# Transposing softmax tiles by VectorE's 32x32 blocks and a round trip through DRAM, in a two-layer decoder trunk

## The chip, the cores and the metric

The kernel runs on one core of a Trainium2 chip. The metric is the device time of one execution in microseconds (us), lower is better. Beside three timed runs there is one profiled execution; all rows below are of that one.

## What is computed

Two layers of a decoder over 256 positions of width 2048, in float32. Each layer has one input projection, several groups of attention heads side by side, a gate and an output projection; 256 memory tokens are attended to as well. The part that matters here is what every head does:

```python
s = jnp.einsum('bhqd,bhkd->bhqk', qi, k).astype(jnp.float32) * scale
s = jnp.where(kpos[None, :] <= qpos[:, None], s, -jnp.inf)
p = jax.nn.softmax(s, axis=-1).astype(v.dtype)
return jnp.einsum('bhqk,bhkd->bhqd', p, v)
```

Layer 0 has 8 latent-attention (MLA) heads, 8 block-sparse (MoBA) heads and 4 memory heads; layer 1 has 16 sliding-window heads with sinks, 6 dilated heads and 4 memory heads. With 256 positions, MoBA's one block is the whole sequence, so those heads are plain causal ones.

## The kernel before, in words

**Weights.** All weight matrices lie in one DRAM array in 332 pieces of up to 512 KB, in the order of use. A piece is loaded on SP's queue into one of RB = 4 `raw` buffers (`issue`, L337), rounded by ScalarE into `hi` (L424) and completed by VectorE with `lo` = raw - hi (L429), into one of HB = 4 pairs. `step` (L538) is the main loop: it converts ahead by AHEAD = 3 pieces (`ensure`), issues the products of half a piece, calls `run_bg` once, and does the same with the second half. A product of a 128x128 weight block is one matmul of `hi` with 512 columns and one of `lo` with 256 (L580, L581); for the projections with the weights as moving operand it is three (L603 to L605).

**Background work.** Everything else, attention included, is written as Python generators. `run_bg` (L495) advances every active generator to its next `yield`, so the `yield`s fix the order of the instructions on each engine. One call of `run_bg` is called a tick here: one half of a piece. At most four queued heads are active together, and a new one starts at the earliest every 5 (later 6) ticks.

**A head.** `g_causal` (L933) makes the scores of a head into one PSUM bank, 384 columns wide: queries 0 to 127 against keys 0 to 127, and queries 128 to 255 against all 256 keys. `g_softmax` (L815) adds the mask and takes the maximum (DVE, L822), the exponential with its sum (ACT, L832), the reciprocal (L839), and scales the two parts (ACT L842, DVE L843). `g_transposed` (L848) transposes the three 128x128 blocks on TensorE with the identity (L850) back into the same bank; ACT rounds two blocks to `hi` in a `PT` buffer (L862) and copies the third (L864), DVE makes `lo` (L866). `pv_causal` (L901) multiplies by the values: three matmuls of 256 columns (L899) and one of 128 in full float32 (L903). `g_meet` (L488) lets a head wait up to 10 ticks so that its PE work falls together with another head's scores.

`g_swa` (L966) does two sliding-window tiles at once (8 such pairs), `g_mem` (L1008) a memory head with four blocks (8 heads). So 38 tiles of three blocks and 8 of four are transposed. `Val` (L905) holds the values of a group of heads; `V.drop` gives them back.

The order on a queue is the order of the code. SP's queue holds the weight loads, each of which waits for DVE's L429 to free a `raw` buffer.

Of the kernel before, what the change touches and what calls it, by code (L numbers as in the profile page):

```python
# [10 lines left out]
F32 = mybir.dt.float32  # L11
# [209 lines left out]
def body(ctx, tc, xr, xT, memT, memr, wall, gains, fing, sinks, consts, out):  # L221
    nc = tc.nc
# [588 lines left out]

    CUTS3 = (slice(0, 128), slice(128, 384))
    CUTS2 = (slice(0, 256), slice(256, 512))

    def g_softmax(sc, cuts, mask, scale, sink, P):  # L815
        s = wtile("st", 8, 16)
        if mask is None:
            nc.vector.tensor_reduce(s[:, 0:2], sc.rearrange("p (t k) -> p t k", t=2),
                                    axis=mybir.AxisListType.X, op=OP.max)
        else:  # L820
            for t, c in enumerate(cuts):
                nc.vector.tensor_tensor_reduce(P[:, c], sc[:, c], mask[:, c], 1.0, -3.0e38, OP.add, OP.max,  # L822
                                               s[:, t:t + 1])
# [5 lines left out]
        yield  # L829
        src = sc if mask is None else P  # L830
        for t, c in enumerate(cuts):
            nc.scalar.activation(P[:, c], src[:, c], AF.Exp, bias=s[:, 2 + t:3 + t], scale=scale,  # L832
                                 accum_out=s[:, 4 + t:5 + t])
# [71 lines left out]
    class Val:  # L905
# [3 lines left out]
        def __init__(self, n, mem=False, u=None):  # L909
            self.n, self.ready, self.given = n, True, u is not None  # L910
            self.us = [u] if self.given else [vr.get() for _ in range(1 + mem)]
            self.parts = [(u[:, 0:512], u[:, 512:1024]) for u in self.us]
            self.second = None if mem else big.get()

# [18 lines left out]
    def g_causal(kt, raws, pe, V, vo, mask, scale, free):  # L933
# [32 lines left out]
    def g_swa(j, q, kc, scale):  # L966
# [22 lines left out]
        while len(ptp.free) < 2:  # L989
            yield  # L990
        PT = [ptp.get() for s in range(2)]
        gs = [g_transposed(P[s], B[s], (0, 1, 2), PT[s], T) for s in range(2)]
        for _ in range(4):
            for g in gs:
                next(g)
            yield
        for s in range(2):
            pv3(B[0][:, 0:256], (vzr[:, 0, s], vzr[:, 1, s]), T[s][0:2], s == 0, False)
        for s in range(2):
            nc.tensor.matmul(B[0][:, 128:256], vz[:, s], T[s][2], start=False, stop=s == 1, skip_group_check=True)  # L1000
        banks.put(B[1])
        for s in range(2):
            pp.put(P[s])
            ptp.put(PT[s])
        yield
        yield from g_finish(j, B[0])

    def g_mem(kt, q, k, V, vo, layer1=False):  # L1008
# [10 lines left out]
        else:  # L1019
            km_drop()  # L1020
        while not (banks.free and pp.free):
            yield
        b, P = banks.get(), pp.get()
        for t in range(2):
# [3 lines left out]
        yield  # L1028
        yield from g_softmax(b, CUTS2, None, 128.0 ** -0.5, None, P)
        while not ptp.free:  # L1030
            yield
        T, PT = [], ptp.get()
        yield from g_transposed(P, b, (0, 2, 1, 3), PT, T)
# [3 lines left out]
        pp.put(P)  # L1037
        ptp.put(PT)
        V.drop()
# [8 lines left out]
    def v_evac(V, c0=0, n=512, r=None):  # L1048
        def evac(m, cur):
            src = [p[:, c0:c0 + n] for p in cur]  # L1050
            hi, lo = (v[:, 0:n] for v in V.parts[0])
# [11 lines left out]

    def vm_split(V, src):
        for t in range(2):
# [169 lines left out]
    def mla_group(g):  # L1235
        V = Val(4)
        h0 = 4 * g
# [168 lines left out]
    def g_last(t, p, lag):  # L1406
# [4 lines left out]
        s = wtile("st", 8, 16)  # L1411
        q = pp.get()
# [3 lines left out]
        nc.scalar.activation(q[:, lo], x[:, lo], AF.Square, accum_out=ss[:, t, 3:4])  # L1416
        nc.vector.tensor_tensor_reduce(q[:, hi], x[:, hi], x[:, hi], 1.0, 0.0, OP.mult, OP.add, ss[:, t, 4:5])
        nc.vector.tensor_reduce(s[:, 0:1], ss[:, t, :], axis=mybir.AxisListType.X, op=OP.add)
# [101 lines left out]
```

## Time and profile before

| what | value |
|---|---|
| three timed runs, median (lowest to highest) | 1004.75 us (1004.57 to 1005.36) |
| the profiled execution, its own time | 1004.67 us |
| its span, first to last instruction | 1002.6 us |
| granted TensorE clock, mean of full speed | 0.999 |
| HBM traffic | 189.38 MB read, 4.19 MB written |

PE stands for TensorE's matmuls, PEld for its weight loads, DVE for VectorE, ACT for ScalarE, POOL for GpSimd, SP for SyncE, which issues DMAs. Matmuls overlap in the pipeline, so the duration of one is longer than the time until the next can start; the pace is read from start to start. Names such as `at` (attention banks in PSUM), `mm` (products of weights) and `P` (score tiles) are the program's, with buffer numbers left out. A line number is that of the kernel before; with the change, the lines behind L271 are higher by 2 and more.

### The profile page before, as it was taken

The numbers are of one execution on the slowest core, as the hardware profiler recorded it, in microseconds if no ns is written. First come the engines' busy times: TensorE is split into PE (matmuls) and PEld (weight loads), VectorE is DVE, ScalarE is ACT, GpSimd is POOL, SyncE is SP. The second block draws the span as 40 slices with busy tenths as digits, with TensorE's granted clock in tenths as the row PEclk, the third lists the DMA queues.
The fourth block names the chain that finished last, engine by engine and source line by source line (L and its number), as shares of the span: only waits on it lengthen the run. The fifth ranks groups of instructions, "written<-read, shape, count | busy, mean of one in ns | idle before, by whom it ended". The sixth has DMA issues, their size and how long they took to land.

```text
span 1002.6 us, 15260 instructions
## 1 busy us (share of the span) xinstructions
PE 993.3 (99%) x5519; PEld 865.2 (86%) x5519; DVE 679.9 (68%) x1326; ACT 602.6 (60%) x1175; POOL 174.0 (17%) x155
## 2 busy tenths in 40 slices
PE   9999999999999999999999999999999999999996
PEld 8888988888888888888888888888899888888885
DVE  7756886887785687765556756777766668666543
ACT  7776776776555456655545555577776565665441
POOL 0000222230241232100000000232211343221110
PEclk9999999999999999999999999999999999999999
DMA  9887455454555555668766554544446555568732
GB/s 337 318 292 246 133 167 187 147 168 168 170 168 171 185 169 170 208 233 268 260 218 231 170 179 168 169 157 158 158 120 201 173 181 165 168 230 282 259 124 84
DMA packets 56093, 194.57 MB, mean 194 GB/s; under 512 B 6481, under 2 KB 8529, under 8 KB 56017
## 3 DMA queue, kind: packets, MB, share of 16 engines
q1 hardware_dynamic: 55296, 192.77, 58.0%
q8 instruction: 43, 0.70, 0.3%
q10 hardware_dynamic: 720, 0.82, 0.2%
q14 instruction: 34, 0.27, 0.1%
HBM read 189.38 MB, written 4.19 MB: 193 GB/s over the span
## 4 chain that ended last, share of the span: by engine, by line
PE 99%; DVE 0%; issue 0%; ACT 0%; DVEq 0%
PE mm L580 38%; PE mm L581 19%; PE mm L603 10%; PE mm L605 10%; PE mm L604 10%; PE at L899 2%; PE at L890 2%; PE at L850 2%; PE at L894 1%; PE mm L1466 1%; PE mm L1464 1%; PE mm L1465 1%; PE at L903 0%; PE at L1079 0%; PE at L1000 0%; PE at L737 0%
## 5 line engine op out<-in xcount | busy, mean ns | idle before, releaser
L429 DVE TENSOR_TENSOR lo<-raw,hi 128x1024 fp32r<-128x1024 f32 (+2 forms) x325 | 394.8, 1217 | 151.9 <-ACT hi L424 147.4
L424 ACT ACTIVATE hi<-raw 128x1024 fp32r<-128x1024 f32 (+2 forms) x325 | 340.5, 1050 | 150.5 <-PE mm L605 103.9
L580 PE MATMUL mm<-bufB,hi 128*128 128x512 f32 x816 | 288.9, 396 | 0.0
L580 PE MATMUL mm<-bufA,hi 128*128 128x512 f32 x816 | 286.5, 394 | 0.0
L581 PE MATMUL mm<-bufB,lo 128*128 128x256 f32 x816 | 229.4, 281 | 0.0
L581 PE MATMUL mm<-bufA,lo 128*128 128x256 f32 x816 | 228.4, 280 | 0.0
L580 PEld LDWEIGHTS mm<-bufB,hi 128*128 128x128 f32 x816 | 154.2, 189 | 34.1 <-ACT hi L398 0.2
L580 PEld LDWEIGHTS mm<-bufA,hi 128*128 128x128 f32 x816 | 153.3, 188 | 32.7
L581 PEld LDWEIGHTS mm<-bufB,lo 128*128 128x128 f32 x816 | 154.3, 189 | 1.0 <-DVE lo L399 0.6
L581 PEld LDWEIGHTS mm<-bufA,lo 128*128 128x128 f32 x816 | 153.4, 188 | 0.2
L603 PE MATMUL mm<-hi,bufB 128*128 128x512 f32 (+1 forms) x264 | 101.7, 385 | 0.0
L604 PE MATMUL mm<-lo,bufB 128*128 128x512 f32 (+1 forms) x264 | 101.2, 383 | 0.0
L605 PE MATMUL mm<-hi,bufB 128*128 128x512 f32 (+1 forms) x264 | 101.1, 383 | 0.0
L616 ACT ACTIVATE tmp<-mm 128x256 f32<-128x256 f32 x118 | 45.1, 382 | 88.8 <-PE mm L581 87.0
L603 PE MATMUL mm<-hi,bufA 128*128 128x512 f32 x204 | 79.8, 391 | 0.0
L604 PE MATMUL mm<-lo,bufA 128*128 128x512 f32 x204 | 79.5, 390 | 0.0
L605 PE MATMUL mm<-hi,bufA 128*128 128x512 f32 x204 | 79.5, 390 | 0.0
L634 POOL TENSOR_TENSOR qk<-qk,cst 32x256 f32<-32x256 f32 x28 | 48.9, 1747 | 162.4 <-DVE rope L633 150.1
L794 POOL TENSOR_TENSOR gf<-gf,qk 128x256 f32<-128x256 f32 x28 | 36.5, 1304 | 159.2 <-ACT e L789 159.2
L605 PEld LDWEIGHTS mm<-hi,bufB 128*128 128x128 f32 x264 | 49.6, 188 | 9.2
L603 PEld LDWEIGHTS mm<-hi,bufB 128*128 128x128 f32 x264 | 49.6, 188 | 9.0
L604 PEld LDWEIGHTS mm<-lo,bufB 128*128 128x128 f32 x264 | 49.6, 188 | 8.6
(188 smaller groups left out, 1101.3 us busy)
## 6 DMA issues: line engine op xcount, KB each, us to landing
raw<-in_wall SPq DMA_DIRECT2D x321, 512.0 KB, 3.5
raw<-in_wall SPq DMA_DIRECT2D x8, 384.0 KB, 3.1
big<-in_xT SPq DMA_DIRECT2D x4, 512.0 KB, 6.3
raw<-in_xr SPq DMA_DIRECT2D x4, 512.0 KB, 5.2
raw<-in_memr SPq DMA_DIRECT2D x4, 512.0 KB, 4.4
big<-in_xr SPq DMA_DIRECT2D x4, 512.0 KB, 5.9
raw<-in_memT SPq DMA_DIRECT2D x4, 512.0 KB, 3.9
x1d<-big SPq DMA_DIRECT2D x4, 512.0 KB, 5.6
```

What stands on the lines that cost most here:

```text
L424: nc.scalar.activation(hi[:, c], raw[:, c], AF.Copy)
L429: nc.vector.tensor_tensor(lo[:, c], raw[:, c], hi[:, c].bitcast(F32), op=OP.subtract)
L580: nc.tensor.matmul(p, hi[:, c], x, start=kt == 0, stop=False, skip_group_check=True)
L581: nc.tensor.matmul(p[:, 0:256], lo[:, c], x[:, 0:256], start=False, stop=last, skip_group_check=True)
L603: nc.tensor.matmul(p, xh, hi[:, w], start=kt == 0, stop=False, skip_group_check=True)
L604: nc.tensor.matmul(p, xh, lo[:, w], start=False, stop=False, skip_group_check=True)
L605: nc.tensor.matmul(p, xl, hi[:, w], start=False, stop=kt == g.kt - 1, skip_group_check=True)
L616: nc.scalar.activation(t, p[:, 256:512], AF.Copy)
L634: nc.gpsimd.tensor_tensor(t[0:n], t[0:n], cs[0:n], op=OP.mult)
L794: nc.gpsimd.tensor_tensor(gf, gf, o_, op=OP.mult)
L850: nc.tensor.transpose(pt[:, 128 * dst:128 * dst + 128], P[:, 128 * b:128 * b + 128], ident)
L890: nc.tensor.matmul(o, q[:, a + q0:a + q0 + 128], k[:, b:b + 256], start=first and i == 0, stop=last and i == 2, skip_group_check=True)
```

## The change

The transposes on TensorE go. The scores' bank is given back as soon as the exponential has read it or the masked scores have been written to `P`. Then, for each tile:

- the scale by 1/sum writes not back into `P` but into one shared tile `W`, in a column order (`keys`, `laid`) that puts key 4i + b of a block into block b's column i;
- DVE transposes `W` in 32x32 blocks into `P` (`g_turn`);
- SP stores `P` to one of 8 DRAM buffers `pd`, and three ticks later loads it back so that each group of 32 partitions is spread over the 128, in four pieces a row;
- four ticks later ACT rounds two blocks from `P` to `hi` in `PT`, DVE makes `lo`, both from SBUF instead of PSUM; the third block is used by the product straight from `P`, as four runs of 32 columns.

A memory head uses two tiles of 256 columns instead of one of 512. The pools change: `P` from 5 of 512 columns to 7 of 384, `PT` from 4 to 3. The values' buffers are taken by `Val.take` only when the values are written, and the first MLA group's lie in a free part of `bufB`. The final normalization uses two `P` tiles where it used one. The core of the diff, without `Val`, the rest of `g_swa`, `g_mem` and `g_last`:

```diff
@@ -269,11 +269,13 @@
     vr = Free("vr", 2, [128, 1024], dt=F32R)
     spl = Free("spl", NSPL, [128, 512], dt=F32R)
     osg = qk
-    pp = Free("P", 5, [128, 512], work)
-    ptp = Free("PT", 4, [128, 512], work, F32R)
+    pp = Free("P", 7, [128, 384], work)
+    ptp = Free("PT", 3, [128, 512], work, F32R)
     banks = Free("at", 4, [128, 512], ps)
     ident = cst[:, C_ID:C_ID + 128]
     x1d = dram.tile([4, 128, 1024], F32, name="x1d")
+    pw = Free("W", 1, [128, 384], work)
+    pds = Free("pd", 8, [128 * 384], dram)
     def wtile(tag, n=256, bufs=2):
         return (small if n < 256 else work).tile([128, n], F32, name=tag, tag=tag, bufs=bufs)
@@ -837,33 +839,86 @@
         if sink is not None:
             nc.vector.tensor_tensor(s[:, 4:6], s[:, 4:6], s[:, 6:8], op=OP.add)
         nc.vector.reciprocal(s[:, 6:8], s[:, 4:6])
-        yield
-        c0, c1 = cuts
-        nc.scalar.activation(P[:, c1], P[:, c1], AF.Copy, scale=s[:, 7:8])
-        nc.vector.tensor_scalar(P[:, c0], P[:, c0], s[:, 6:7], None, op0=OP.mult)
-        yield
-        yield
-        yield
-    def g_transposed(P, pt, blocks, T, out):
-        for dst, b in enumerate(blocks):
-            nc.tensor.transpose(pt[:, 128 * dst:128 * dst + 128], P[:, 128 * b:128 * b + 128], ident)
-        n = 128 * len(blocks)
-        if n == 512:
-            while not spl.free:
+        yield s[:, 6:8]
+    def laid(w, n):
+        return w.rearrange("p (b s i) -> p s b i", b=4, s=n)
+    def keys(P):
+        return P.rearrange("p (s i b) -> p s b i", b=4, i=32)
+    def g_turn(P, W, n):
+        nc.vector.transpose(P[:, 0:128 * n], W)
+        yield
+        d = pds.get()
+        c = d[0:128 * 128 * n]
+        nc.sync.dma_start(c.rearrange("(p f) -> p f", p=128), P[:, 0:128 * n])
+        for _ in range(3):
+            yield
+        nc.sync.dma_start(P[:, 0:128 * n].rearrange("p (a f) -> p a f", a=4),
+                          c.rearrange("(a p f) -> p a f", a=4, p=128))
+        pds.put(d)
+        for _ in range(4):
+            yield
+    def g_causal_T(P, r, out):
+        while not pw.free:
+            yield
+        w = pw.get()
+        nc.scalar.activation(laid(w, 3)[:, 1:3], keys(P[:, 128:384]), AF.Copy, scale=r[:, 1:2])
+        nc.vector.tensor_scalar(laid(w, 3)[:, 0], keys(P[:, 0:128])[:, 0], r[:, 0:1], None, op0=OP.mult)
+        yield
+        pw.put(w)
+        yield from g_turn(P, w, 3)
+        while not ptp.free:
+            yield
+        PT = ptp.get()
+        hi, lo = PT[:, 0:256], PT[:, 256:512]
+        p = P.rearrange("p (a s j) -> p s a j", a=4, s=3)
+        parts = [v.rearrange("p (s a j) -> p s a j", a=4, s=2) for v in (hi, lo)]
+        out.append((hi, lo, p[:, 2], PT))
+        nc.scalar.activation(parts[0], p[:, 0:2], AF.Copy)
+        yield
+        nc.vector.tensor_tensor(parts[1], p[:, 0:2], parts[0].bitcast(F32), op=OP.subtract)
+        yield
+        yield
+    def g_mem_T(P, r, out):
+        gs = []
+        for t in range(2):
+            while not pw.free:
                 yield
-            hi, lo = T, spl.get()
-            out.append((hi, lo))
-        else:
-            hi, lo = T[:, 0:256], T[:, 256:512]
-            out.append((hi, lo, P[:, 256:n]))
-        m = hi.shape[-1]
-        yield
-        nc.scalar.activation(hi, pt[:, 0:m], AF.Copy)
-        if m < n:
-            nc.scalar.activation(P[:, m:n], pt[:, m:n], AF.Copy)
-        yield
-        nc.vector.tensor_tensor(lo, pt[:, 0:m], hi.bitcast(F32), op=OP.subtract)
+            w = pw.get()
+            if t:
+                nc.scalar.activation(laid(w[:, 0:256], 2), keys(P[t][:, 0:256]), AF.Copy, scale=r[:, 1:2])
+            else:
+                nc.vector.tensor_scalar(laid(w[:, 0:256], 2), keys(P[t][:, 0:256]), r[:, 0:1], None, op0=OP.mult)
+            yield
+            pw.put(w)
+            gs.append(g_turn(P[t], w[:, 0:256], 2))
+            next(gs[t])
+        for i in range(9):
+            for g in gs:
+                next(g, None)
+            if i < 8:
+                yield
+        while not (ptp.free and spl.free):
+            yield
+        hi, lo = ptp.get(), spl.get()
+        p = [P[t][:, 0:256].rearrange("p (a s j) -> p s a j", a=4, s=2) for t in range(2)]
+        parts = [v.rearrange("p (s t a j) -> p t s a j", t=2, s=2, a=4) for v in (hi, lo)]
+        out.append((hi, lo))
+        for t in range(2):
+            nc.scalar.activation(parts[0][:, t], p[t], AF.Copy)
+        yield
+        for t in range(2):
+            nc.vector.tensor_tensor(parts[1][:, t], p[t], parts[0][:, t].bitcast(F32), op=OP.subtract)
         yield
         yield
...
@@ -949,16 +1010,19 @@
         for t in free:
             qk.put(t)
         yield
-        yield from g_softmax(b, CUTS3, mask, scale, None, P)
+        T = []
+        for r in g_softmax(b, mask, scale, None, cuts3(P)):
+            if r is None:
+                yield
+        banks.put(b)
+        yield from g_causal_T(P, r, T)
         yield from g_meet()
-        while not ptp.free:
-            yield
-        T, PT = [], ptp.get()
-        yield from g_transposed(P, b, (0, 1, 2), PT, T)
-        yield from g_meet()
+        while not banks.free:
+            yield
+        b = banks.get()
         pv_causal(b, V.head(vo), T[0])
         pp.put(P)
-        ptp.put(PT)
+        ptp.put(T[0][3])
         V.drop()
         yield
         yield from g_finish(kt, b)
...
@@ -980,30 +1044,32 @@
         spl.put(R[0])
         qk.put(q)
         yield
-        gs = [g_softmax(B[s], CUTS3, lay[:, 512:896], scale, j + 8 * s, P[s]) for s in range(2)]
-        for _ in range(6):
-            for g in gs:
-                next(g)
...
```

**PE's queue, in the first MLA group**, before. `at` are attention banks, `P` score tiles, `bufB,hi` and `bufB,lo` weight products; L850 are the transposes of two heads, L894 and L890 the scores of the third:

```order
L580 MATMUL mm<-bufB,hi 128x512
L581 MATMUL mm<-bufB,lo 128x256
L850 MATMUL at_125<-cst,P_117 128x128 x3
L850 MATMUL at_123<-cst,P_113 128x128 x3
L894 MATMUL at_124<-qk_92,qk_94 128x128
L894 MATMUL at_124<-qk_97,qk_98 128x128
L890 MATMUL at_124<-spl_112,spl_111 128x256 x3
L890 MATMUL at_124<-bufA,spl_109 128x256 x3
L580 MATMUL mm<-bufB,hi 128x512
```

And with the change, the scores of the same third head:

```order
L582 MATMUL mm<-bufB,hi 128x512
L583 MATMUL mm<-bufB,lo 128x256
L949 MATMUL at_125<-qk_92,qk_94 128x128
L949 MATMUL at_125<-qk_97,qk_95 128x128
L945 MATMUL at_125<-spl_111,spl_109 128x256 x3
L945 MATMUL at_125<-bufA,spl_112 128x256 x3
L582 MATMUL mm<-bufB,hi 128x512
```

The six transposes are gone, and the weight products go on right behind the scores. (Lines 580 and 581 are now 582 and 583, L894 and L890 are L949 and L945.)

**SP's queue with the change, in the MoBA heads.** `pd` is DRAM; a row with x3 is three loads of weight pieces:

```order
L339 DMA raw<-in_wall 128x1024 x7
L859 DMA pd_129<-P_115 128x384
L339 DMA raw<-in_wall 128x1024
L862 DMA P_115<-pd_129 128x4x96
L339 DMA raw<-in_wall 128x1024 x3
L859 DMA pd_130<-P_116 128x384
L339 DMA raw<-in_wall 128x1024
L862 DMA P_116<-pd_130 128x4x96
```

Before there were only weight loads here. Each store (L859) now has one weight load between itself and the load back (L862), and three weight loads stand behind that one before the next head's store.

## Rows read from the trace of the kernel before

**Rows 1.** The page: the span, and each engine's busy time, share and instructions.

```profile
span 1002.6 us, 15260 instructions
...
PE 993.3 (99%) x5519; PEld 865.2 (86%) x5519; DVE 679.9 (68%) x1326; ACT 602.6 (60%) x1175; POOL 174.0 (17%) x155
```

**Rows 2.** The chain that ended last, whole span: shares by line.

```profile
by line: PE mm L580 37.7%; PE mm L581 19.2%; PE mm L603 10.5%; PE mm L605 10.4%; PE mm L604 10.4%; PE at L899 1.9%; PE at L890 1.9%; PE at L850 1.6%; PE at L894 1.0%; PE mm L1466 0.8%; PE mm L1464 0.8%; PE mm L1465 0.8%; PE at L903 0.5%; PE
```

**Rows 3.** Waits of PE: who waited for whom, us in total, times, longest.

```profile
PE at L1079 <- DVE ones L1073: 1.0, 1, 1.0
```

**Rows 4.** PE's timeline from 200 us: start us, us, engine, line, operation.

```profile
203.27 0.39 PE L580 MATMUL mm<-bufB,hi 128*128 128x512 f32 x1
...
204.66 0.39 PE L580 MATMUL mm<-bufB,hi 128*128 128x512 f32 x1
```

**Rows 5.** L850: count, ns min/median/max, first and last start us.

```profile
L850 PE MATMUL at<-cst,P x146: 270/273/273, 118.7 to 894.1; 128*128 128x128 f32 x146
```

**Rows 6.** The chain by time, two stretches: start us, us, what.

```profile
191.66 0.65 PE at L850 x6
...
200.41 0.36 PE at L899 x3
201.00 0.36 PE at L899 x3
...
353.42 0.36 PE at L899 x3
...
365.69 0.33 PE at L850 x3
```

**Rows 7.** Lines by form, costliest first: busy us, mean ns, idle before.

```profile
L429 DVE TENSOR_TENSOR lo<-raw,hi 128x1024 fp32r<-128x1024 f32 x315 | 385.8, 1227 | 148.8 <-ACT hi L424 144.2 <-PE mm L580 2.8
L424 ACT ACTIVATE hi<-raw 128x1024 fp32r<-128x1024 f32 x315 | 332.6, 1058 | 149.7 <-PE mm L605 103.9 <-PE mm L580 36.6 <-DMA raw<-in_wall 4.1
...
L842 ACT ACTIVATE P<-P,st 128x256 f32<-128x256 f32 x46 | 22.3, 503 | 4.3 <-DVE st L839 3.4
...
L822 DVE CUSTOM_DVE_ANT_0 P<-at,lay 128x256 f32<-128x256 f32 x38 | 15.9, 420 | 0.0
...
L866 DVE TENSOR_TENSOR PT<-at,PT 128x256 fp32r<-128x256 f32 x38 | 14.9, 416 | 0.9 <-ACT P L864 0.7
L862 ACT ACTIVATE PT<-at 128x256 fp32r<-128x256 f32 x38 | 14.7, 386 | 24.8 <-PE at L850 24.8
...
L822 DVE CUSTOM_DVE_ANT_0 P<-at,lay 128x128 f32<-128x128 f32 x38 | 11.0, 290 | 39.7 <-PE at L890 39.7
...
L864 ACT ACTIVATE P<-at 128x128 f32<-128x128 f32 x38 | 10.7, 281 | 0.0
...
L633 DVE STREAM_SHUFFLE rope<-qk 128x256 f32<-128x256 f32 x14 | 6.2, 446 | 0.0
```

**Rows 8.** Busy us by stretch: PE, PEld, DVE, ACT, POOL, PE clock, DMA share, GB/s.

```profile
200.00:300.00 100.00, 100.00 (x589) 88.46 (x588) 76.36 (x175) 61.18 (x133) 25.69 (x21) 1.00 0.52 169
650.00:780.00 130.00, 130.00 (x829) 116.53 (x828) 92.26 (x254) 90.14 (x226) 32.10 (x26) 1.00 0.51 160
```

**Rows 9.** DMA: queues (packets, MB, share), then issues (count, KB, us to landing).

```profile
q1 hardware_dynamic: 55296, 192.77, 58.0%
...
q10 hardware_dynamic: 720, 0.82, 0.2%
...
raw<-in_wall SPq DMA_DIRECT2D x321, 512.0 KB, 3.5
...
big<-in_memT SPq DMA_DIRECT2D x3, 512.0 KB, 6.5
...
out<-big SPq DMA_DIRECT2D x6, 128.0 KB, 2.5
```

**Rows 10.** Waits of all engines, longest first in total.

```profile
ACT hi L424 <- PE mm L605: 103.9, 79, 1.7
...
ACT hi L424 <- DMA raw<-in_wall: 4.7, 6, 2.0
```

More of the change, by code (lines that the diff above doesn't have):

```diff
@@ L810, in gate_evac, with cuts3, g_softmax @@
         return evac
-    CUTS3 = (slice(0, 128), slice(128, 384))
-    CUTS2 = (slice(0, 256), slice(256, 512))
-    def g_softmax(sc, cuts, mask, scale, sink, P):
+    def cuts3(P):
+        return [(c, P[:, c]) for c in (slice(0, 128), slice(128, 384))]
+    def g_softmax(sc, mask, scale, sink, Ps):
         s = wtile("st", 8, 16)
@@ L820, in g_softmax @@
         else:
-            for t, c in enumerate(cuts):
-                nc.vector.tensor_tensor_reduce(P[:, c], sc[:, c], mask[:, c], 1.0, -3.0e38, OP.add, OP.max,
+            for t, (c, P) in enumerate(Ps):
+                nc.vector.tensor_tensor_reduce(P, sc[:, c], mask[:, c], 1.0, -3.0e38, OP.add, OP.max,
                                                s[:, t:t + 1])
@@ L829, in g_softmax @@
         yield
-        src = sc if mask is None else P
-        for t, c in enumerate(cuts):
-            nc.scalar.activation(P[:, c], src[:, c], AF.Exp, bias=s[:, 2 + t:3 + t], scale=scale,
+        for t, (c, P) in enumerate(Ps):
+            nc.scalar.activation(P, sc[:, c] if mask is None else P, AF.Exp, bias=s[:, 2 + t:3 + t], scale=scale,
                                  accum_out=s[:, 4 + t:5 + t])
@@ L909, in __init__, with take @@
         def __init__(self, n, mem=False, u=None):
-            self.n, self.ready, self.given = n, True, u is not None
-            self.us = [u] if self.given else [vr.get() for _ in range(1 + mem)]
+            self.n, self.ready, self.given, self.mem = n, True, u is not None, mem
+            self.us = [u] if self.given else []
+        def take(self):
+            while len(vr.free) + len(self.us) < 1 + self.mem or not (self.mem or big.free):
+                yield
+            while len(self.us) < 1 + self.mem:
+                self.us.append(vr.get())
             self.parts = [(u[:, 0:512], u[:, 512:1024]) for u in self.us]
-            self.second = None if mem else big.get()
+            self.second = None if self.mem else big.get()
         def head(self, c):
@@ L982, in g_swa @@
         yield
-        gs = [g_softmax(B[s], CUTS3, lay[:, 512:896], scale, j + 8 * s, P[s]) for s in range(2)]
-        for _ in range(6):
-            for g in gs:
-                next(g)
+        gs = [g_softmax(B[s], lay[:, 512:896], scale, j + 8 * s, cuts3(P[s])) for s in range(2)]
+        for i in range(3):
+            r = [next(g) for g in gs]
+            if i < 2:
+                yield
+        for b in B:
+            banks.put(b)
+        for s in range(2):
+            launch(g_causal_T(P[s], r[s], T))
+        while len(T) < 2:
+            yield
+        for _ in range(3):
             yield
         yield from g_meet()
-        while len(ptp.free) < 2:
+        while not banks.free:
             yield
[L991 to L995, printed above, removed]
-            yield
+        b = banks.get()
         for s in range(2):
-            pv3(B[0][:, 0:256], (vzr[:, 0, s], vzr[:, 1, s]), T[s][0:2], s == 0, False)
+            pv3(b[:, 0:256], (vzr[:, 0, s], vzr[:, 1, s]), T[s][0:2], s == 0, False)
         for s in range(2):
-            nc.tensor.matmul(B[0][:, 128:256], vz[:, s], T[s][2], start=False, stop=s == 1, skip_group_check=True)
-        banks.put(B[1])
+            nc.tensor.matmul(b[:, 128:256], vz[:, s], T[s][2], start=False, stop=s == 1, skip_group_check=True)
         for s in range(2):
             pp.put(P[s])
-            ptp.put(PT[s])
+            ptp.put(T[s][3])
         yield
-        yield from g_finish(j, B[0])
+        yield from g_finish(j, b)
     def g_mem(kt, q, k, V, vo, layer1=False):
@@ L1020, in g_mem @@
             km_drop()
-        while not (banks.free and pp.free):
+        while not banks.free or len(pp.free) < 2:
             yield
-        b, P = banks.get(), pp.get()
+        b, P = banks.get(), [pp.get(), pp.get()]
         for t in range(2):
@@ L1028, in g_mem @@
         yield
-        yield from g_softmax(b, CUTS2, None, 128.0 ** -0.5, None, P)
-        while not ptp.free:
+        T = []
+        Ps = [(slice(256 * t, 256 * t + 256), P[t][:, 0:256]) for t in range(2)]
+        for r in g_softmax(b, None, 128.0 ** -0.5, None, Ps):
+            if r is None:
+                yield
+        banks.put(b)
+        yield from g_mem_T(P, r, T)
+        while not banks.free:
             yield
-        T, PT = [], ptp.get()
-        yield from g_transposed(P, b, (0, 2, 1, 3), PT, T)
+        b = banks.get()
         for h in range(2):
@@ L1036, in g_mem @@
         spl.put(T[0][1])
-        pp.put(P)
-        ptp.put(PT)
+        for p in P:
+            pp.put(p)
+        ptp.put(T[0][0])
         V.drop()
@@ L1049, in evac @@
         def evac(m, cur):
+            yield from V.take()
             src = [p[:, c0:c0 + n] for p in cur]
@@ L1064, in vm_split @@
     def vm_split(V, src):
+        yield from V.take()
         for t in range(2):
@@ L1415, in g_last @@
             nc.vector.tensor_tensor(x[:, c], p[:, c], x[:, c], op=OP.add)
-        nc.scalar.activation(q[:, lo], x[:, lo], AF.Square, accum_out=ss[:, t, 3:4])
-        nc.vector.tensor_tensor_reduce(q[:, hi], x[:, hi], x[:, hi], 1.0, 0.0, OP.mult, OP.add, ss[:, t, 4:5])
+        nc.scalar.activation(q, x[:, lo], AF.Square, accum_out=ss[:, t, 3:4])
+        nc.vector.tensor_tensor_reduce(q1, x[:, hi], x[:, hi], 1.0, 0.0, OP.mult, OP.add, ss[:, t, 4:5])
         nc.vector.tensor_reduce(s[:, 0:1], ss[:, t, :], axis=mybir.AxisListType.X, op=OP.add)
```

4 lines of the change are left out of this document (2 added, 2 removed).

## The prediction

> **What bounds the kernel now.** I read the profile from the top down: the engines' busy time, the chain that ended last, the waits of the engine that the chain names, and then the places that the change touches. TensorE (PE) is busy 993.3 us of the 1002.6 us span, VectorE (DVE) 68%, ScalarE (ACT) 60% [rows 1]. The chain is PE for 99%; 88% of it, by five lines, is the weight products, and the transposes of L850 have 1.6% [rows 2]. PE's list of waits holds one entry, of 1.0 us at the start [rows 3]. So from start to tail PE runs one instruction after another, and the time is the sum of what PE issues. A product of a piece (512 columns, then 256) starts every 0.35 us: four pairs from 203.27 to 204.66 [rows 4]. That is 1.39 us for half a piece, which is one turn of the background generators; I call it a tick. Inserted attention products lengthen a tick, so 1.39 us is its lower bound.
>
> **What is removed.** 38 score tiles of three blocks (22 causal heads, 16 sliding-window tiles) and 8 memory tiles of four are transposed: 38 x 3 + 8 x 4 = 146, the count in the trace [rows 5]. The 273 ns there is no price: it contains the pipeline. The chain shows the pace: six take 0.65 us, three 0.33 us [rows 6]. That is 0.11 us each, 146 x 0.11 = 16.0 us; the chain's 1.6% of 1002.6 us gives the same. Nothing covers these on PE, and all lie on the path. The order of PE with the change is otherwise that of before: as many weight products, nowhere a longer run of attention work without them, and the queue of heads ends earlier.
>
> **What is added.** (1) DVE: 38 block transposes of 384 columns and 16 of 256. The nearest row is the shuffle of 128x256, 446 ns; two rows of L822 grow by 130 ns for 128 columns more, so 384 take about 0.58 us [rows 7]. Sum 38 x 0.58 + 16 x 0.45 = 29 us. Bounds: nothing below the 290 ns of a 128-column operation (16 us), and twice the estimate above (58 us). I take 29, as the shuffle is nearest in kind. (2) The scale by 1/sum now writes W in another column order, reading every fourth element: between ACT's 503 ns of today [rows 7] and twice that, 38 x 0.5 = 19 us more on ACT over the kernel. I take no more, since the count of elements is the same. (3) ACT loses 38 copies of the third block, 281 ns each, 10.7 us [rows 7]. All this lies beside PE: in the stretch from 200 to 300 us DVE has 24 us idle of 100 and ACT 39, in the sliding-window stretch 38 and 40 of 130 [rows 8]. Seven heads in the first of them add 4 us to DVE, 8 us at the upper bound. Cost on the path: nothing, as long as PE's operands are ready. (4) The third block is now read by PE as four runs of 32 columns. The trace has no such operand; that product takes 0.23 us now (from 200.77 to 201.00) [rows 6]. Bounds: nothing, and one more of the same for 38 products, 8.7 us; no row gives a reason for a gain. I take nothing, as equal columns have cost equal time in every row.
>
> **The round trip.** 54 stores of 196 or 131 KB, and 54 loads that cut each row into four pieces of 384 or 256 B: 128 and 512 packets. All go on SP's queue among the weight loads. A store waits for its block transpose; the load waits until the store has landed, and whatever stands behind it on SP waits too. From the code, the load is issued three ticks behind the store, ACT's copy of the loaded tile comes four ticks behind the load, the product that uses it three ticks later: ten ticks, at least 13.9 us, in causal and memory heads, three more in a sliding-window pair.
>
> No DRAM round trip of this kind stands in the trace. The landings nearest in bytes are 2.5 us (128 KB out) and the longest of common ones 6.5 us (512 KB in) [rows 9]. With ACT's copy and DVE's subtraction (0.4 us each [rows 7]) two landings come to 5.8 to 13.8 us, under the 13.9 at both ends; I take 2.5 and 3.5 us, 6.8 us. While SP stands at the load, weight loads stand behind it; their margin comes next. ACT works ahead of PE: it converts piece i+3 during step i and is held by PE, 103.9 us at one line, against 4.7 us by weight DMA [rows 10]. Of the three pieces ahead, 8.3 us, a conversion takes 2.3 (L424, L429 [rows 7]). So ACT can stand still for some 6 us before PE lacks weights, and a raw buffer's refill (3.5 us [rows 9]) has about as much to spare.
>
> Packets: the 55,296 on q1 took 58.0% of 16 engines' span, 168 ns each at 3.5 KB; the 720 on q10, of 1.1 KB, 45 ns each [rows 9]. A load of 512 packets takes 512 x 45 / 16 = 1.4 us of all engines at the lower price and 5.4 us at the upper one. I take 45 ns: the pieces are nearer to 1.1 KB. A causal head comes every 12.3 us (353.42 to 365.69 [rows 6]); the DMA is busy half of that [rows 8], and gets 1.4 us plus about 0.4 for the store: under 70%. At 168 ns (5.4 and 1.3 us) the transfers come to 13 of 12.3 us, saturated. The Trainium skill speaks against such pieces: "DMA: Bandwidth & Descriptors", Specifications, gives 512 B as the least transfer at line rate, with a read-modify-write below. By the 45 ns of the row the sum is 988.7 us; by the rule, taken as hard as the row of the long packets allows, it is the second rival's 1015.7. No run here shows it yet.
>
> **Sum.** 1004.67 us of the profiled execution (0.08 below the median of the runs) minus 16.0 = 988.7 us. The 2.1 us outside the span, PE's start and the tail behind its last product stay.
>
> **Rivals.**
> - *Part of the gain is lost* (chance 0.16, of which 0.02 ends within 0.2%). PE now waits a little where it does not wait today: the strided operand costs up to 8.7 us, or weights come late after SP stood at a load. With 38 groups of tiles, 0.2 us each is 7.6 us: 996 us. For it: PE has no other slack than what ACT and DVE work ahead. Against: PE waits for nobody today, and ACT hardly for weights [rows 3, 10].
> - *The round trip is too long* (0.12, slower). The place is the product behind the copy of the loaded tile, in the 30 causal and memory heads. It decides from two landings together of 13.1 us on, which a saturated DMA at 168 ns a packet would give. At 7 us each the product waits 0.9 us, 30 x 0.9 = 27 us: 1015.7 us. Break-even is 16.0 / 30 = 0.53 us of wait per head. ACT, standing at the copy, would also hold up the weights. Against: the DMA was idle 48% of these stretches, and weight loads landed in 3.5 us there.
> - *The change does not reach PE* (0.02, within 0.2%). The gaps that transposes filled reappear as waits of the same products. Against: PE's order has weight products there, whose weights lie ready: 1004.7 us.
>
> **Numbers.** Forecast 988.7 us, chance 0.70, by itself 986 to 991: below, if PE's pace in a transpose also cost neighbours up to 0.02 us; above, for a first few waits. Left: 0.16, 0.12 and 0.02. A difference of 0.2% (2 us) is what a measurement can tell here. Faster: 0.70 + 0.14 = 0.84. Same: 0.02 + 0.02 = 0.04. Slower: 0.12. The range goes from 986 to 1000 us, taking in the strided operand's upper bound and the 0.2 us waits, and leaves out the slow rival, the unchanged one and a little of the second.
>
> **What would show it.** Right: the transposes' 1.6% gone from the chain, PE's waits still about 1 us, the load's landing under 5 us, ACT's wait for the loaded tile small, DVE near 710 us and ACT near 590 us busy. Wrong: PE waiting for DVE or ACT at L899 or L903 (their new numbers), weight conversions waiting for DMA far above 4.7 us, landings of 7 us or more, a DMA share near full in the attention stretches, or a product of 128 columns of well over 0.23 us.

## The result, and the profile after

The changed kernel takes 990.4 us (median of four runs, 990.09 to 990.49) against 1004.77 us (1004.57 to 1005.36) before: a ratio of 0.9855 [0.9838, 0.9873]. It is 14.4 us faster, and 1.7 us above the 988.7 us forecast. The profiled execution took 990.38 us.

The page of the changed kernel: span, busy times, the weight queue, HBM traffic. It answers to [rows 1, 9].

```profile
span 988.6 us, 15244 instructions
...
PE 976.3 (99%) x5373; PEld 847.4 (86%) x5373; DVE 718.2 (73%) x1388; ACT 605.0 (61%) x1137; POOL 169.3 (17%) x155
...
q1 hardware_dynamic: 91584, 211.92, 66.0%
...
HBM read 198.95 MB, written 13.76 MB: 215 GB/s over the span
```

PE issues 146 instructions less and is busy 17.0 us less, but the span is only 14.0 us shorter: 3.0 us more of it are gaps. PE's waits in the changed kernel (who for whom: us in total, times, longest), which answer to [rows 3], say where:

```profile
PE at L1153 <- DVE ones L1147: 1.0, 1, 1.0
PE mm L582 <- ACT hi L400: 0.7, 2, 0.5
PE mm L583 <- DVE lo L431: 0.6, 1, 0.6
PE mm L582 <- ACT big L1127: 0.6, 1, 0.6
PE at L954 <- DVE spl L921: 0.6, 1, 0.6
PE mm L583 <- DVE lo L401: 0.5, 2, 0.2
```

The first was there before. Those at L400, L401 and L431 lie in the first 14 us, among the first weights; they came out larger or smaller in every kernel below. The other two are new: L954 at 133.6 us, L1127 at 190.3 us. Behind them PE has no listed wait to its last product. The chain that ended last, 99% PE before, is now 93% PE: it leaves PE in the first 14 us and on its way to both places.

**A balance by stages.** Three PE instructions are the same in every version: the first product that broadcasts a statistic (L667 before, L669 now), the first transpose of the residual at the layer boundary (L737, L739), and the last product of the program. The first two enclose layer 0 with 64 of the 146 transposes (16 heads of three, 4 of four), the last two layer 1 with 82. Their start times in PE's timeline, in us:

| kernel | statistic | boundary | last product | layer 0 | layer 1 |
|---|---|---|---|---|---|
| before | 71.28 | 544.99 | 994.00 | 473.71 | 449.01 |
| after | 71.49 | 540.23 | 980.08 | 468.74 | 439.85 |
| only PE's transposes left out (e1) | 71.38 | 538.74 | 978.59 | 467.36 | 439.85 |
| memory heads two ticks later (e6) | 71.40 | 539.01 | 978.84 | 467.61 | 439.83 |
| and causal scale a tick later (e10) | 71.52 | 538.24 | 978.07 | 466.72 | 439.83 |

Layer 1 gains 9.16 us, 0.112 us for each of its transposes, and loses nothing: the same 439.85 as with the transposes simply left out. Layer 0 gains 4.97 us where 64 x 0.11 = 7.0 were due. The 2 us that are missing lie at the two new waits and at a shorter stand behind the first, as e6 and e10 below show by taking them away.

**The two waits.** ACT's timeline of the changed kernel around the second (start us, us, engine, line, operation, idle before and its releaser), then PE's and DVE's around both, from the same view:

```profile
186.98 0.76 ACT L873 ACTIVATE W<-P,st 128x256 f32<-128x256 f32 x1 [2.22 <-DVE st L841]
...
190.06 0.58 ACT L1127 ACTIVATE vr<-mm 128x512 fp32r<-128x512 f32 x1
...
190.28 0.28 PE L583 MATMUL mm<-bufB,lo 128*128 128x256 f32 x1
191.18 0.50 PE L582 MATMUL mm<-bufB,hi 128*128 128x512 f32 x1 [0.62 <-ACT big L1127]
191.52 0.28 PE L583 MATMUL mm<-bufB,lo 128*128 128x256 f32 x1
...
131.31 1.41 DVE L628 TENSOR_TENSOR bufA<-qk,bufA 64x256 fp32r<-64x256 f32 x2
132.75 0.76 DVE L921 TENSOR_TENSOR spl<-P,PT 128x256 fp32r<-128x256 f32 x2
...
132.73 0.28 PE L954 MATMUL at<-PT,vr 128*128 128x256 f32 x1
133.57 0.39 PE L954 MATMUL at<-spl,vr 128*128 128x256 f32 x1 [0.55 <-DVE spl L921]
...
142.64 0.28 PE L954 MATMUL at<-PT,vr 128*128 128x256 f32 x1
143.01 0.39 PE L954 MATMUL at<-spl,vr 128*128 128x256 f32 x1
```

At 186.98 ACT's scale (L873) had stood 2.22 us for DVE's reciprocal (L841). Before, a `yield` lay between the two, and the scale waited 0.57 us for it; the diff removes that `yield`. Behind the scale on ACT comes the eviction of the value products (L1127), 1.5 us later than before (190.06 against 188.56), and PE waits for the PSUM bank that it empties. At 132.75 DVE makes the low parts of a memory head (L921), late behind L628, in two operations that take 0.76 us together; PE has begun the product that needs them. DVE is nearly full here: busy 22.4 of the 23 us from 121 to 144 us, against 20.4 before.

The list counts a wait from the end of the instruction before it. From start to start more is lost. Behind 190.28 the next product starts 0.90 us later instead of 0.12, and the one after that 0.34 instead of 0.23: 0.9 us. At 132.73 the next start comes 0.84 us later instead of 0.12, with 0.1 more behind it: 0.8 us. The next memory head loses another 0.35 us in the same way at 142.64, which is too short for the list.

**The added work by line.** Lines by form (busy us, mean ns; idle before):

```profile
L873 ACT ACTIVATE W<-P,st 128x256 f32<-128x256 f32 x38 | 28.6, 753 | 22.1 <-DVE st L841 12.8 <-DVE P L855 9.1
L855 DVE STREAM_TRANSPOSE P<-W 128x384 f32<-128x384 f32 x38 | 21.7, 571 | 5.3 <-ACT W L873 4.8
L887 DVE TENSOR_TENSOR PT<-P,PT 128x256 fp32r<-128x256 f32 x38 | 16.8, 450 | 1.5 <-ACT PT L885 1.4
L874 DVE TENSOR_SCALAR W<-P,st 128x128 f32<-128x128 f32 x38 | 16.5, 435 | 1.1
L885 ACT ACTIVATE PT<-P 128x256 fp32r<-128x256 f32 x38 | 15.4, 411 | 21.2 <-PE at L954 14.6 <-DMA P<-pd 6.6
...
L855 DVE STREAM_TRANSPOSE P<-W 128x256 f32<-128x256 f32 x16 | 7.1, 441 | 1.7 <-ACT W L899 1.6
```

The block transposes took 571 and 441 ns, sum 28.8 us. The strided scale took 753 ns against the 503 of [rows 7], the strided DVE one (L874) 435. The product that reads four runs of 32 columns, by its line's view (ns min, median, max), and its pace in the chain, of a head before and a head now:

```profile
L958 PE MATMUL at<-P,big x44: 270/273/275, 200.4 to 891.8; 128*128 128x128 f32 x44
...
338.98 0.22 PE at L903 x2
...
340.06 0.22 PE at L958 x2
```

L903 before had 271/273/275 ns. The pace, and layer 1 at 439.85 us with this operand as in e1 without it, say the same: the strided operand costs nothing.

**The round trip.** DMA issues (count, KB, median us to landing), to be set beside [rows 9]:

```profile
raw<-in_wall SPq DMA_DIRECT2D x321, 512.0 KB, 4.2
pd<-P SPq DMA_DIRECT2D x38, 192.0 KB, 4.0
P<-pd SPq DMA_DIRECT2D x38, 192.0 KB, 3.8
```

Store and load together take 7.8 us, and weight loads 4.2 where they took 3.5. ACT waits 6.9 us in all for a loaded tile (6.6 in the row of L885 above, 0.3 in the memory heads). The queue's share rose from 58.0% of 1002.6 us to 66.0% of 988.6: times 16 engines, 1136 us more for 36,288 more packets, 31 ns each if all of it is put down to them. The stretches of [rows 8] now (PE, PEld, DVE, ACT, POOL, clock, DMA share, GB/s):

```profile
200.00:300.00 100.00, 100.00 (x581) 88.25 (x580) 82.51 (x185) 63.11 (x127) 26.21 (x21) 1.00 0.62 196
650.00:780.00 130.00, 130.00 (x803) 115.36 (x802) 107.01 (x267) 89.93 (x203) 31.11 (x28) 1.00 0.67 209
```

### The profile page after: what moved, and what is told of

The parts are those of the page before. It is cut to its first block, busy times and chain, and to the rows that moved or that the text cites. A ratio compares the mean times of both kernels' runs of the same rounds, so it can differ in the third digit from the quotient of the medians.

```text
span 988.6 us, 15244 instructions
## 1 busy us (share of the span) xinstructions
PE 976.3 (99%) x5373; PEld 847.4 (86%) x5373; DVE 718.2 (73%) x1388; ACT 605.0 (61%) x1137; POOL 169.3 (17%) x155
## 4 chain that ended last, share of the span: by engine, by line
PE 93%; DVE 2%; ACT 1%; issue 1%; DMA 1%; POOL 0%; SPq 0%; DVEq 0%; ACTq 0%; POOLq 0%
PE mm L582 35%; PE mm L583 18%; PE mm L605 11%; PE mm L606 10%; PE mm L607 10%; PE at L954 2%; PE at L945 2%; PE at L949 1%; PE mm L1540 1%; PE mm L1538 1%; PE mm L1539 1%; DVE lo L431 1%; DMA big<-in_memT 1%; PE at L958 0%; PE at L1067 0%
## 5 line engine op out<-in xcount | busy, mean ns | idle before, releaser
L431 DVE TENSOR_TENSOR lo<-raw,hi 128x1024 fp32r<-128x1024 f32 (+2 forms) x325 | 394.2, 1217 | 129.7 <-ACT hi L426 126.5
L834 ACT ACTIVATE P<-P,st 128x128 f32<-128x128 f32 x76 | 33.9, 448 | 26.3 <-DVE st L828 15.0
```

The lines of the kernel that those rows point to most:

```text
L431: nc.vector.tensor_tensor(lo[:, c], raw[:, c], hi[:, c].bitcast(F32), op=OP.subtract)
L834: nc.scalar.activation(P, sc[:, c] if mask is None else P, AF.Exp, bias=s[:, 2 + t:3 + t], scale=scale, accum_out=s[:, 4 + t:5 + t])
```

## The experiments

Each was run beside the kernel before on the same chip; its median there was 1004.6 us (e1 to e4), 1004.66 (e5 to e8) and 1004.95 (e9 to e11).

### e1: what PE's transposes cost

In the kernel before, the transposes are left out; the products then use whatever lies in the bank.

```diff
-        for dst, b in enumerate(blocks):
-            nc.tensor.transpose(pt[:, 128 * dst:128 * dst + 128], P[:, 128 * b:128 * b + 128], ident)
```

> The kernel before with the transposes of L850 left out and nothing in their place: ACT and DVE round the untransposed scores, so the products use other data. Theory (PE's pace): the transposes cost PE 146 x 0.11 = 16.0 us and nothing covers them: 1004.8 - 16.0 = 988.8 us, within 0.5. The change then lost 1.6 us of this in three small waits. Rival (order): the change gained from its new order and its pools too, and the transposes are worth less: 991 us or more here. Rival (the missing 1.7 us is the pace): a transpose costs PE less than 0.11 us, 14.3 / 146 = 0.098: 990.4 us here.

Measured 989.44 us (989.35 to 989.66), ratio 0.9849 [0.9834, 0.9864]: 15.2 us less, 0.104 each. One wait is new:

```profile
PE at L680 <- ACT qk L782: 0.5, 1, 0.5
```

From start to start this stand (at 128.5 us, in layer 0) costs 0.63 us. With it given back, layers 0 and 1 gain 6.35 + 0.63 + 9.16 = 16.1 us, against the 16.0 of the sum. The whole gain comes from PE's queue. The changed kernel is within 1 us of this run, or 1.6 us if its stand is left out: all that the change adds costs PE no more than that.

### e2: what the round trip costs

In the changed kernel the store and the load are left out, so the tiles stay as the block transposes left them; the ticks stay.

```diff
-        nc.sync.dma_start(c.rearrange("(p f) -> p f", p=128), P[:, 0:128 * n])
...
-        nc.sync.dma_start(P[:, 0:128 * n].rearrange("p (a f) -> p a f", a=4),
-                          c.rearrange("(a p f) -> p a f", a=4, p=128))
```

> The changed kernel without the 54 stores and 54 loads: the block-transposed tile is used as it stands, so the products use other data; every tick, DVE's block transposes and the order on PE stay. Theory (PE's pace): the round trip lies beside PE, and its removal gives at most the 0.6 us wait for the memory head's operand: 989.8 to 990.4 us. Rival (round trip on the path): the 1.7 us missing from the forecast are DMA contention and waits for landings: 988.7 us, and if these also hid in PE's pace, below 988.

Measured 990.62 us (989.97 to 990.94), ratio 0.986 [0.9845, 0.9874]: the same as with it. PE's two waits stay (lines are lower by 3):

```profile
PE mm L582 <- ACT big L1124: 0.6, 1, 0.6
...
PE at L951 <- DVE spl L918: 0.5, 1, 0.5
```

So neither wait is the DMA's, and 19.15 MB more on the queue are free here.

### e4: smaller pieces

The load in three DMAs, with pieces of 128 B instead of 384 or 256 B (in memory heads, two DMAs):

```diff
-        nc.sync.dma_start(P[:, 0:128 * n].rearrange("p (a f) -> p a f", a=4),
-                          c.rearrange("(a p f) -> p a f", a=4, p=128))
+        for s in range(n):
+            nc.sync.dma_start(P[:, 0:128 * n].rearrange("p (a s f) -> p a s f", a=4, s=n)[:, :, s],
+                              c.rearrange("(a p s f) -> p a s f", a=4, p=128, s=n)[:, :, s])
```

> The changed kernel with each load cut into three (memory: two) loads of 128 B pieces: 74,752 packets in place of 27,648. The changed kernel's 36,288 packets more than before took 31 ns each of one engine. Theory (packets are cheap and lie beside PE): 47,104 x 31 ns / 16 = 91 us of all engines more, the share goes from 66% to about 75%, and the time stays: 990.4 us, within 1. Rival (the packet price of the long ones, 168 ns): 495 us more, the DMA full, landings of 7 us and more, and the products wait: above 1010 us.

Measured 990.56 us (990.34 to 990.6), ratio 0.986 [0.9844, 0.9876]: unchanged. The queue of weights and round trips, from the page:

```profile
q1 hardware_dynamic: 140160, 211.92, 68.8%
```

48,576 more packets raise the share by 2.8 points, not by the 9 expected at 31 ns a packet: extra packets of the same bytes are cheaper still. The price of a packet is nowhere near the 168 ns that the second rival needed.

### e11: the load right behind the store

The load comes one tick behind the store instead of three, the copy stays where it was.

```diff
-        for _ in range(3):
-            yield
+        yield
...
-        for _ in range(4):
+        for _ in range(6):
             yield
```

> The changed kernel with the load one tick behind the store instead of three, and the copy where it was, so that SP stands at the load for most of the store's landing of 4.0 us while weight loads stand behind it. Order on PE, DVE and ACT unchanged. Theory (a weight load has some 5 us to spare): SP's wait at the load grows from 43 us in total to 100 to 160, and the time stays, 990.4 us within 1. Rival (weights come late, PE waits for their conversion): 995 us or more, with ACT's wait for weight DMA well above 6 us.

Measured 990.11 us (989.98 to 990.2), ratio 0.9854 [0.9837, 0.987]. The waits of SP's queue, then of ACT for weights:

```profile
SPq L861 <- DMA pd<-P: 129.1, 46, 5.1
...
ACT hi L426 <- DMA raw<-in_wall: 26.2, 19, 3.0
```

They were 42.6 and 6.2 us in the changed kernel. SP stands 86 us longer at the loads, ACT waits 20 us more for weights, and PE's time doesn't move. But SP's waits in all stay the same (811 us, now 809): those in front of weight loads (L339) fall from 691 to 608 us. SP would have stood for a `raw` buffer anyway, so this shows that the stands at the load are harmless here, not that weights can come 86 us later.

### e3 and e8: the ticks in front of ACT's copy

The four ticks between load and copy go behind the copy (e3), or two of them (e8); product and load stay where they were. Memory heads are changed alike. e3:

```diff
         pds.put(d)
-        for _ in range(4):
-            yield
...
         nc.scalar.activation(parts[0], p[:, 0:2], AF.Copy)
-        yield
+        for _ in range(5):
+            yield
```

> The changed kernel with the four or five ticks between the load and ACT's copy moved behind the copy: ACT stands at the copy until the load has landed, all else stays in its order. A landing takes 3.8 us (median of the changed kernel's loads). Theory (PE's pace, ACT has 6 us in hand): ACT stands 2 to 4 us in each of 38 groups, its list of waits shows 80 to 150 us at the copy, PE waits for weights only where two stands follow each other closely: 990.4 to 995 us. Rival (no margin): what ACT stands, PE stands, 38 x 2 us or more: above 1060 us.

> The changed kernel with two of the ticks between load and copy moved behind the copy (none moved: 990.4 us; all moved: 1114.4 us, where ACT waited 6.3 us on average at 29 copies, and SP issued the load some 4 us after ACT had come to the copy). Theory (the wait is landing plus SP's lag behind ACT, less the ticks; PE waits for what exceeds ACT's 6 us in hand): two ticks, 2.8 us, take the wait from 6.3 to 3.5 us, and PE waits little: 990 to 996 us. Rival (each microsecond that ACT stands costs PE one, by proportion): about half of 124 us, 1040 to 1065 us.

Measured: e3 1114.38 us (1113.35 to 1117.08), ratio 1.1097 [1.108, 1.1113]; e8 1017.76 us (1013.8 to 1020.77), ratio 1.0129 [1.0101, 1.0156]. The waits of e3:

```profile
ACT PT L883 <- DMA P<-pd: 183.0, 29, 8.7
...
PE at L954 <- DVE PT L886: 22.0, 14, 2.6
...
PE mm L582 <- ACT hi L426: 15.6, 9, 3.1
PE mm L583 <- DVE lo L431: 10.6, 16, 1.1
PE mm L582 <- ACT big L1127: 8.1, 2, 4.9
```

One head of e3 on ACT and on SP, from the timeline:

```profile
305.50 0.42 ACT L883 ACTIVATE PT<-P 128x256 fp32r<-128x256 f32 x1 [7.43 <-DMA P<-pd]
...
298.06 0.42 SPq L859 DMA_DIRECT2D pd<-P  x1
300.54 0.33 SPq L339 DMA_DIRECT2D raw<-in_wall  x1
302.00 0.38 SPq L862 DMA_DIRECT2D P<-pd  x1
```

ACT stood from 298.07 to 305.50. SP came to the load only at 302.00, behind a weight load at 300.54 and the landing of the store, and the load landed 3.5 us later. So ACT's stand is SP's lag and the landing together, which my theory had left out. The time is that of the rival, above 1060 us, though not by its rule: PE lost about half of what ACT stood. And the stand reached PE not as missing weights alone (15.6 us): the largest entry is the attention product waiting for the low part, and a PSUM bank takes 8.1.

PE's page line in e8; the spans of the profiled executions are 1019.0 us (e8, the longest of its four runs) and 1112.0 us (e3; PE busy 1023.2):

```profile
PE 987.4 (97%) x5373; PEld 853.5 (84%) x5373; DVE 720.5 (71%) x1388; ACT 603.8 (59%) x1143; POOL 167.6 (16%) x155
```

Gaps grew from 12.3 us to 31.6 (e8) and 88.8 (e3); busy PE grew by 11.1 and 46.9 us for the same instructions, at a mean granted clock of 0.991 and 0.963. ACT stood 118 and 224 us for loaded tiles, and the spans grew by 30 and 123 us: a quarter of it, then a half. Neither the hidden nor the proportional price of the expectations of e8 holds. Between these two runs the price of a us on ACT rises with the length of the stand (3.4 us on average at the causal copies in e8, 6.3 in e3).

### e9: three turns for one

Each block transpose is issued three times.

```diff
-        nc.vector.transpose(P[:, 0:128 * n], W)
+        nc.vector.transpose(P[:, 0:128 * n], W)
+        nc.vector.transpose(P[:, 0:128 * n], W)
+        nc.vector.transpose(P[:, 0:128 * n], W)
```

> The changed kernel with every block transpose on DVE issued three times over (same source and target): 57.6 us more on DVE (2 x 28.8), 776 us busy, 79% of the span; in the sliding-window stretch 107 of 130 us become 125. Theory (DVE lies beside PE, with two places of layer 0 where it is just late): 990.4 us plus up to 2 us at the memory heads of layer 0. Rival (DVE is close to being the bound, so that each microsecond more at a head reaches PE): above 1000 us.

Measured 1005.5 us (1004.3 to 1008.13), ratio 1.0005 [0.9996, 1.0014]: 57 us more of DVE work (2 x 28.8) cost 15 us, the whole gain. The rival held. The largest waits of PE:

```profile
PE at L669 <- DVE rb L664: 4.0, 1, 4.0
PE mm L583 <- DVE lo L431: 3.8, 2, 2.1
PE mm L605 <- DVE qk L620: 1.2, 1, 1.2
```

The span of the profiled execution is 15.8 us longer: PE's gaps grew by 8.7 us, and its busy time by 7.1 for the same instructions. Behind the waits of 4.0 and 2.1 us the granted clock fell for a while (0.63 from 132 to 136 us, in the mean 0.994). DVE is busy 774.6 us, 77% of the span. That it has 23% left doesn't make its work free: a head's operations come in a burst (DVE is busy 38.3 of the 40 us from 120 to 160 us), and what stands behind them is a statistic or a low part that PE wants next.

### e5, e6, e7, e10: giving the two waits back

e5 puts back a tick between reciprocal and scale for all tiles (and makes the loop of the sliding-window pairs one step longer to match). e6 gives memory heads two ticks more before their product. e7 is both. e10 is e6 and e5 without e5's tick in memory heads (those without a mask).

```diff
         nc.vector.reciprocal(s[:, 6:8], s[:, 4:6])
+        yield
         yield s[:, 6:8]
```

```diff
         yield from g_mem_T(P, r, T)
+        yield
+        yield
         while
```

> The changed kernel with one tick between the reciprocal and the scale, as the kernel before has it. In the changed kernel ACT waited 2.2 us for the reciprocal at 187 us, wrote the values of the second MLA group 1.5 us later than before, and PE waited for that bank at 190.3 us (0.8 us). Theory (the missing tick holds ACT up): that wait goes, 0.8 us: 989.6 us. Rival (the longer scale, 753 instead of 503 ns, and the new places of ACT's work hold the values up): the wait stays, 990.4 us or, with heads a tick longer, more.

> The changed kernel with two ticks more between DVE's lo of a memory head and the product that uses it. In the changed kernel PE waited 0.55 us for DVE there at 133.6 us, once; without the round trip this wait stayed (0.5 us), so it is DVE's own lateness. Theory: the wait goes and nothing else moves: 989.8 us. Rival (the later product only moves the wait, to the values' buffers or the next bank): 990.4 us or more.

> Both edits together. Theory: the two waits were independent and both go, 1.4 us: 989.0 us, level with the kernel before without its transposes (989.4) within 0.4. Rival: they share a cause (DVE and ACT too busy in that part of layer 0), and the waits come up elsewhere: 990 us or more.

> The changed kernel with the tick before the scale for the masked heads alone (the memory heads, whose lateness cost PE 3.4 us of waits and a slow clock when that tick was given to them too, stay as they are) and the two ticks before the memory heads' product. Theory (the two waits in layer 0 are independent): 989.1 us of the second edit alone less the 0.8 us wait for the values: 988.3 us. Rival (the tick moves heads on and brings another wait): 989.1 us or more.

| run | us, median (range) | ratio | wait at 133.6 | wait at 190.3 |
|---|---|---|---|---|
| e5 | 994.03 (992.17 to 994.26) | 0.989 [0.9874, 0.9907] | 2.2 us | gone |
| e6 | 989.12 (989.0 to 989.68) | 0.9847 [0.9832, 0.9862] | gone | 0.6 us |
| e7 | 989.63 (988.87 to 989.89) | 0.985 [0.9835, 0.9864] | gone | gone |
| e10 | 989.5 (989.27 to 989.78) | 0.9848 [0.9833, 0.9863] | gone | gone |

By the table of stages, e6 wins back 1.13 us of layer 0, and e10 another 0.89, which are the losses from start to start named above. Weight product by weight product, the changed kernel lies 0.09 us behind e6 until 130 us and 1.22 from 148 us to the layer boundary; e6 lies 0.12 us ahead of e10 until 186 us and 0.78 behind it from 194 us on. Nothing else of layer 0 moved. e10's layers together are 16.17 us under those of before: nothing of the gain is missing any more. In the measured time e10 misses the 988.3 us expected and is not ahead of e6, though its last product starts 0.77 us earlier: from there to the end of the span it took 9.4 us against 8.6, all of it behind the issue of the last output stores. It ran on another chip, where the kernel before took 0.3 us more; what makes this tail longer stays open. e6, the shortest measured, is 1.3 us below the changed kernel, with ranges that don't meet. e7 keeps a new wait of 1.1 us of the statistic's product for DVE (L669).

e5 is the instructive miss. Its tick made a memory head's product late (L955, 2.2 us), and the statistic's product waited as in e7. Then, in PE's timeline of e5 and the stretches around it (columns as in [rows 8]):

```profile
138.06 0.39 PE L955 MATMUL at<-spl,vr 128*128 128x256 f32 x1 [2.23 <-DVE spl L922]
...
139.52 0.63 PE L582 MATMUL mm<-bufA,hi 128*128 128x512 f32 x1
139.95 0.41 PE L583 MATMUL mm<-bufA,lo 128*128 128x256 f32 x1
140.16 0.63 PE L582 MATMUL mm<-bufA,hi 128*128 128x512 f32 x1
```

```profile
136.00:140.00 4.00, 1.95 (x13) 1.85 (x14) 3.96 (x7) 4.00 (x9) 1.72 (x2) 0.93 0.80 238
140.00:144.00 4.00, 4.00 (x18) 3.49 (x17) 3.96 (x8) 2.30 (x9) 0.94 (x1) 0.65 0.69 230
```

Five pairs of products, 139.52 to 142.72, start 0.64 us apart instead of the 0.35 of [rows 4], with a granted clock of 0.65 from 140 to 144: the engine ran part of it at the lower of its two levels, 1.2 GHz, after standing for 2.2 us. That is 5 x 0.29 = 1.5 us behind a wait of 2.2. It isn't always that much: in e8, behind a wait of 2.1 us, seven pairs from 651.31 to 655.79 us start 0.64 us apart (clock 0.55 and 0.59 in the two stretches of 4 us from 649), 2.0 us; in e9, behind 1.7 us, the clock stays at 1.00.

## Why the prediction was right

**The removed term** was 146 x 0.11 = 16.0 us. The stages give 16.1 us in e1 and 16.2 in e10. The pace read from the chain, and not the 273 ns of an instruction, was the price.

**The signs.** L850 is gone from the chain, the load lands in 3.8 us, and ACT's wait for it is small, as forecast. One sign of being wrong was there too: PE waited at L954, the new number of L899. PE's waits came to 4.0 us instead of about 1, with DVE and ACT busier than the 710 and 590 us named.

**Term (1), DVE's turns,** was 0.58 and 0.45 us, sum 29; measured 0.571 and 0.441, sum 28.8. DVE came to 718.2 us and not 710, since L874 takes 435 ns for a row of 306 before (4.9 us), now with every fourth float read and runs of 32 written; L887 and L921, which now read `P` in runs of 32 from SBUF, take 1.9 and 3.4 us more. Why these two do was not tested.

**Term (2), the strided scale,** is the one that was mis-sized: taken at 503 ns as before, "since the count of elements is the same". It takes 753 ns, 1.5 times as much, inside the bound of twice. 38 x 0.25 = 9.5 us more on ACT eat up most of the 10.7 us of term (3), and the memory heads' scale (761 ns) and the copies from SBUF the rest, so that ACT is busy 605.0 us and not near 590. On the path this cost nothing by itself.

**Term (4), the strided operand:** nothing, as taken; the 8.7 us of the upper bound are refuted by L958's pace and by layer 1. The reason given, equal time for equal columns in every row, was thin: in [rows 6] 128 columns take 0.11 us at L850 and 0.23 at L903, which runs as two instructions.

**Landings** were taken as 2.5 + 3.5 = 6.0 us and took 4.0 + 3.8 = 7.8: nearest in bytes was too low. These share the queue with the weights, which may be why; no run had a round trip without weight loads. Both ends lay under ten ticks, so the conclusion stood. A DMA share of "under 70%" was 62 to 67%.

**The packets** decided the second rival. By the 45 ns of the row it was off; measured were 31 ns. The Trainium skill's "DMA: Bandwidth & Descriptors", Specifications, puts the least transfer at line rate at 512 B, with a read-modify-write below; 27,648 pieces of 384 and 256 B, and in e4 pieces of 128 B, cost this kernel no time that its runs show (990.4, 990.56, and 990.62 without any). The rule may hold for the transfer itself; no run here measured it on an empty queue.

**The 1.7 us above the forecast** are the first rival's mechanism at a small size: PE waits where it did not wait before, but not for the strided operand nor for weights. By the stages: 1.13 us at 133.6 and 142.6 us, 0.89 us at 190.3 us, 0.21 us at the start; less 0.17 by which the transposes were worth more than 16.0, 0.08 in the tail and 0.29 outside the span (1.8 us now, 2.1 before), that is 1.7. I had seen neither place: the prediction followed the tile through its ten ticks, and not the `yield` that went between the reciprocal and the scale, nor how full DVE's queue is when it comes to the memory heads' low parts.

**Two sentences of the reasoning were too generous,** though the result didn't hang on them. "ACT can stand still for some 6 us before PE lacks weights": when it did (e3, e8), PE paid at stands of 3.4 us on average already, through the low parts of attention tiles, PSUM banks and a lower clock. What protects the change is that ACT hardly ever stands for a tile (6.9 us in all), and this the four ticks in front of the copy buy: without them it is 110 us slower than before. And DVE's upper bound, twice the turns, was costed at nothing since DVE has idle time. At three times (e9) it costs 15 us; twice was not tried.

## What to carry to other kernels

When one engine is busy without gaps, work taken off it is worth its pace from start to start, as long as the replacement has ticks enough between its steps: a DRAM round trip of 8 us was free with ten ticks and cost 124 us when ACT stood for it. Follow every `yield` that an edit removes, not only the steps that it adds: one of the two places that took back 2 us of 16 came from an operation that now follows too closely on another engine's. The other came from a short operation on a helper whose queue was full just there; two ticks more took it away. The idle share of a helper engine says little of what it can take on; issuing the added work several times over shows it.

## What the runs showed that I had not expected

- ACT reading every fourth float and writing runs of 32: 753 ns for 128x256 against 503 contiguous; DVE's scale of 128x128, 435 against 306. PE reading four runs of 32 columns: no difference (0.22 us a head in the chain).
- After a stand of 2.2 us PE's products ran at 0.64 us a pair instead of 0.35 for 3.2 us, at a granted clock of 0.65: here the wait cost two thirds more than itself, in e8 one of 2.1 us about as much again. The 0.6 us waits of the changed kernel show no such stretch.
- Pieces of 128 B instead of 384 and 256 added 48,576 packets and 2.8 points of the queue's share: 443 us of 16 engines, 9 ns each.
